# Loads and order of work in the head of a hybrid S5 / short-convolution layer

## The chip, the cores and the metric

The kernel runs on one core of one Trainium2 chip. The metric is device microseconds of one execution. TensorE (PE; its weight loads are listed as PEld), VectorE (DVE), ScalarE (ACT), GpSimd (POOL) and SyncE (SP) each work through an instruction list of their own, in order; the kernel is written so that the order of calls in the source is the order on every engine. Copies between device memory and the on-chip memory are issued by SP, ACT or POOL and run beside the engines.

## The reference, cut to what matters

One layer on a latent stream x (512 tokens by 2048 channels) and a context of 256 tokens:

```
shift, scale, gate = split(silu(c) @ w_ada + b_ada)       # the same with c_ctx for the context
h  = layernorm(x)   * (1 + scale)   + shift
hc = layernorm(ctx) * (1 + scale_c) + shift_c
u, z_s5, v, bg, cg, z_cv = split(h @ w_in);   u_c = hc @ w_in[:, :1024]
y_s5 = glu(s5_scan_both_directions(u, u_c))               # diagonal complex state space, 64 groups
y_cv = bg * conv3(cg * v)
x = layernorm(alpha * x + gate * (concat(y_s5 * silu(z_s5), y_cv * silu(z_cv)) @ w_out)) * ln_g + ln_b
```

All arithmetic is float32. A product with w_in, w_glu or w_out is made of three matmuls in a rounded format: both operands are split into a rounded part (hi) and the rest (lo), and hi·hi, lo·hi and hi·lo are summed.

## The kernel before, in words

The 2048 channels are 16 blocks of 128, numbered k. **The head** (`head`, line 461) makes the modulated, split input of every block (`hhi[k]`, `hlo[k]` for the 512 latent tokens, `chi[k]`, `clo[k]` for the 256 context tokens) and, in the same pass, the part of the input projection that needs the context: `lat` adds block k to three banks of latent u (9 matmuls of 512 columns), `cxt` to half of the context u (12 matmuls of 256 columns). A weight piece serves `cxt` for one half `hf` of the columns, and `lat` too where `hf` is 0; `half` (line 695) does one piece, two per k.

Rows of x and ctx come as six tiles of 128 rows (q = 0 to 3 of x, 4 and 5 of ctx). `stats` (524) takes mean and variance, `norm` (536) normalises in place, `turn` (554) transposes all 16 blocks through PSUM into `xl[k]` and `xc[k]`. The scale and shift of a block come from w_ada in 1 MB pieces (k, hf): `ada` (571) multiplies one piece with silu(c) in eight matmul calls that appear as 16 rows, into the tile `aps`; when both halves are in, `combine` (596) copies it (ACT, `part`), transposes it on PE into `cps`, reduces it on DVE into `ss[k]` and adds the bias `bss`. `aps` and `cps` are the two halves of one PSUM tile, and a write waits for the reads of the whole tile. `mod` (609) then computes hi on ACT and the two DVE steps that give lo.

The 1 MB pieces of w_ada and the four x tiles share a ring `wa` of RB = 7 buffers; the ctx tiles come as sixteen 128 KB pieces in another ring. `ada_ahead` (495) issues a piece of w_ada on POOL (the first on ACT) as soon as a buffer of the ring is given back. Weight pieces of 256 KB (`raw`, five buffers) are issued on SP by `load` (207). `ahead(i)` (214) splits the pieces up to two ahead of item i: `whi` on ACT, `wlo` on DVE, three buffers of each.

From k = 4 on a loop (705) repeats: `ada(k, 0)`, a `half`, `ada(k, 1)`, the first step of `combine`, a `half`, then `some(2.6)`, then the rest of `combine`, then `mod` for both streams. `some` (686) runs a stretch of `s5_params` (305): some two hundred small DVE steps that compute the discretised state-space parameters, cut at the `yield` lines; it stops when the planner's DVE clock has moved on by the given microseconds. Its sine and cosine, its quadrant step and its first power are blocks of around 20 instructions without a `yield`. Near its end it waits for the flag that `ada(13, 0)` is issued (then two ring buffers are free), transposes a table through `cps` in four steps and writes it to device memory (`Wd`). After the loop the last pieces run, then three u tiles are written out (`put_u`).

**The body** follows: 260 more items (256 KB weight pieces, nearly all with 12 matmuls of 512 columns) for the rest of the input projection, then the GLU, then the output projection. Beside them run background generators: `phase_w` (963, state inputs, from `Wd` and `bt`), the scan, `phase_y` (1086, outputs of the scan), `g_load` (1222) and the gate. The planner (`_Clock`, `_Timed`) keeps an estimated time for every engine and tile while the program is written; a background step is placed after the item at which the PE's estimated time has passed the estimated time of what it needs (`until`, `later`). Line 122 estimates when a copy has landed. The first GLU item (838) requires all of `g_load`.

Of the kernel before, what the change touches and what calls it, by code (L numbers as in the profile page):

```python
# [74 lines left out]
class _Timed:  # L75
# [26 lines left out]
    def __getattr__(self, what):  # L102
        f = getattr(self._e, what)

        def call(*a, **k):
            c, e = self._c, self._n
            out = a[0]
            ins = [x for x in list(a[1:]) + list(k.values()) if hasattr(x, "shape")]
            start = max([c.t[e]] + [c.free(out) - 0.13] + [c.ready(x) - (0.13 if c.who.get(c.key(x)) == e else 0.0) for x in ins])
            if what == "dma_start":  # L110
                if e == "pool":
                    c.t[e] = max(c.t[e], start - 1.5) + 1.0
                else:
                    c.t[e] = start if e == "sp" else c.t[e] + 0.5
                    c.hw = max(c.hw, min(start, c.t["pe"])) + 0.45
                    start = max(start, c.hw)
                n = 4
                for d in out.shape:
                    n *= d
                n *= min(2.0, max(1.0, 190.0 / min(out.shape[-1], ins[0].shape[-1]))) / 350e3  # L120
                c.bw = max(c.bw, min(start, c.t["pe"])) + n
                end = max(start + n, c.bw) + (4.0 if e == "pool" else 2.0)
            else:
                if e == "dve" and any(c.key(x) == c.last for x in ins):
                    start += 0.12
# [12 lines left out]

        return call
# [3 lines left out]
def tile_hybrid_s5_shortconv(  # L143
# [8 lines left out]
    ve, ac = _Timed(nc.vector, "dve", clk), _Timed(nc.scalar, "act", clk)  # L152
# [25 lines left out]
    def cslot(name, dt=F32):  # L178
        return hcp.tile([P, CTX], dt, name=name, tag="hc", bufs=32)
# [11 lines left out]
    def tt(out, a, b, op, e=None):  # L191
        (e or ve).tensor_tensor(out, a, b, op=op)
# [268 lines left out]
    def head():  # L461
        with pool(name="head", bufs=1) as hp, \
# [10 lines left out]
            ve.memset(epst, EPS)  # L473


            xt = {}

            def load_x(q):
                if q < 4:
                    t = hp.tile([P, D], F32, name="xt", tag="wa", bufs=RB)  # L480
                    n = 4 if q == 0 else 1
                    for f in range(n):
                        c = slice(f * D // n, (f + 1) * D // n)
                        sp.dma_start(t[:, c], x_in[q * P:(q + 1) * P, c])
                    xt[q] = [t[:, f * 512:(f + 1) * 512] for f in range(4)]
                else:
                    xt[q] = [cslot("xt") for _ in range(8)]
                    for f, t in enumerate(xt[q]):
                        sp.dma_start(t, ctx_in[(q - 4) * P:(q - 3) * P, f * CTX:(f + 1) * CTX])

            order = [(k, hf) for k in range(KT) for hf in range(2)]
            wa = {}
            nload = 0

            def ada_ahead(n):
                nonlocal nload
                while nload < min(n, len(order)):
                    t = hp.tile([P, D], F32, name="wa", tag="wa", bufs=RB)
                    (ac if nload == 0 else gp).dma_start(t, wada_ss[order[nload]])
                    wa[order[nload]] = t.rearrange("p (k c) -> p k c", k=8)  # L500
                    nload += 1

            for q in range(4):
                load_x(q)
            ada_ahead(RB - 4)
            for _ in range(2):
                load()
            for q in (4, 5):
                load_x(q)
            load()  # L510
            lam = hp.tile([P, 3, NG], F32, name="lam")
            for t, src in ((bss, b_ss), (lam, lam_in), (cvw, cv_w), (cvb, cv_b), (bgl, b_glu), (dsk, dsk_in)):
                sp.dma_start(t, src)
            acc = [ps.tile([P, 512], F32, name=f"acc{i}") for i in range(7)]
            aps = ps.tile([P, 512], F32, name="aps")
            aps, cps = aps[:, 0:256], aps[:, 256:512]
# [5 lines left out]
            sts, rss = {}, {}  # L522

            def stats(q):
                n = len(xt[q])
                stt = hp.tile([P, 8, 6], F32, name="bst", tag="bst", bufs=2)
                mv = hp.tile([P, 2], F32, name="mv", tag="mv", bufs=3)
                for f in range(n):
                    ve.bn_stats(stt[:, f], xt[q][f])
                    yield  # L530
                ve.bn_aggr(mv, stt[:, 0:n])
                sts[q] = mv
                rss[q] = rstd_a(hp, mv[:, 1:2], epst)
                yield

            def norm(q):
                yield from rstd_b(rss[q], sts[q][:, 1:2])
                for f, t in enumerate(xt[q]):
                    if q < 4:
                        if f:  # L540
                            break
                        t = bass.AP(tensor=t.tensor, offset=t.offset, ap=[t.ap[0], [1, D]])
                    ve.tensor_scalar(t, t, sts[q][:, 0:1], rss[q][:, 3:4], op0=OP.subtract, op1=OP.mult)

            def run(*gs):
                gs = list(gs)
# [5 lines left out]
                            gs.remove(g)  # L552

            def turn(q):
                w = 512 if q < 4 else CTX
                for k4 in range(4):
                    b = acc[(4 * q + k4) % 7 if q < 4 else 3 + k4]
                    for k in range(4):
                        c = (k4 * 4 + k) * P
                        pe.transpose(b[:, k * P:(k + 1) * P], xt[q][c // w][:, c % w:c % w + P], ident)  # L560
                    for k in range(4):
                        kk = k4 * 4 + k
                        dst = xl[kk][:, q * P:(q + 1) * P] if q < 4 else xc[kk][:, (q - 4) * P:(q - 3) * P]
                        if q == 5 and k % 2:
                            ve.tensor_copy(dst, b[:, k * P:(k + 1) * P])
                        else:
                            ac.activation(dst, b[:, k * P:(k + 1) * P], AF.Copy)
                if q < 4:
                    ada_ahead(RB - 3 + q)

            def ada(k, hf):
                w = wa.pop((k, hf))
                for j in range(8):
                    pe.matmul(aps[32 * (j % 4):32 * (j % 4) + 32], cs[:, hf * 8 + j], w[:, j],
                              start=hf == 0 and j < 4, stop=hf == 1 and j > 3)
                ada_ahead(2 * k + hf + RB + 1)
                done.add((k, hf))

            def lat(k, whi, wlo):
                lh, ll = hhi[k], hlo[k]  # L580
# [25 lines left out]
                ve.tensor_scalar(s[:, 1], s[:, 1], 1.0, None, op0=OP.add)  # L606
                yield

            def mod(k, x, his_, los_, new, m):
                his_[k], los_[k] = new("hi", F32R), new("lo", F32R)  # L610
                sh, sc = ss[:, k, 0, m:m + 1], ss[:, k, 1, m:m + 1]
                ac.activation(his_[k], x[k], AF.Identity, scale=sc, bias=sh)
                ve.tensor_scalar(x[k], x[k], sc, sh, op0=OP.mult, op1=OP.add)
                tt(los_[k], x[k], his_[k].bitcast(F32), OP.subtract)

            def mod_l(k):
                mod(k, xl, hhi, hlo, slot, 0)

            def mod_c(k):
                mod(k, xc, chi, clo, cslot, 1)  # L620

            def split(n):
                while st["split"] < n:
# [5 lines left out]
                    his[j] = (hi, lo)  # L629
                    st["split"] += 1  # L630

            done = set()
            run(stats(0))
            run(norm(0))
            run(stats(1))
# [45 lines left out]
            mod_l(3)  # L681
            mod_c(3)
            st["pos"] = 3
            params = s5_params(hp, cps, lam, lambda: (13, 0) in done)

            def some(us):
                t0 = ck["dve"]
# [16 lines left out]

            for k in range(4, KT):
                ada(k, 0)
                half()
                if k == 4:
                    half()
                ada(k, 1)  # L710
                next(comb[k])
                half()
                some(2.6)
                next(comb[k])
                mod_l(k)
                mod_c(k)
            while st["pos"] < 2 * KT:
                half()
                some(2.6)
# [742 lines left out]
```

## Time and profile before

| | |
|---|---|
| median of 3 runs | 1085.43 us (1080.07 to 1087.07) |
| profiled execution | 1081.24 us, span 1079.5 us |
| mean granted TensorE clock | 0.948 of full |
| busy: PE, PEld, DVE, ACT, POOL | 952.0, 764.4, 680.4, 374.3, 146.1 us |
| device memory | 179 GB/s mean over the span |

Busy time is what an engine's instructions took in the profiled execution, and the granted clock of 1.00 is 2.4 GHz, 0.50 is 1.2 GHz. PE is busy for 88% of the span, but not evenly: of the page's forty slices (27 us each) the second to ninth show it at 5 to 8 tenths, and the twelfth to the last but one at 8 or 9 tenths.

### The profile page before, as it was taken

Reading aid. Unit: us, or ns where it says so; the run is one execution under the profiler, and the core shown is the slowest. Engines: PE = TensorE matmul, PEld = TensorE weight load, DVE = VectorE, ACT = ScalarE, POOL = GpSimd, SP = SyncE. Lnnn points to the kernel's source line nnn. Section 1 sums busy time; section 2 is a strip of 40 time slices with the busy share of each in tenths; the row PEclk is TensorE's granted clock in tenths of the full one; section 3 lists DMA queues with packets and bytes.
Section 4 is the critical chain, followed back from the end, with each engine's and each line's share of the span. In section 5 each row is a group of like instructions: output and inputs, shape, how many; then the busy total and the mean of one; then the engine's idle time right before and its main releaser. Section 6 shows DMA issues by size and latency. Waiting matters only on the chain.

```text
span 1079.5 us, 15402 instructions
## 1 busy us (share of the span) xinstructions
PE 952.0 (88%) x5488; PEld 764.4 (71%) x5488; DVE 680.4 (63%) x1562; ACT 374.3 (35%) x669; POOL 146.1 (14%) x272
## 2 busy tenths in 40 slices
PE   1577776789699989999999999999989999999990
PEld 1455554568588877888888888888878887778780
DVE  4645555543487877898885667464124787982666
ACT  2432222223144334222424545444534442222321
POOL 1101003001011110000002021201020013300044
PEclk9879888789799999999999999999999999999996
DMA  9937555228999992333346364738397778945512
GB/s 326 377 121 281 206 185 216 79 59 197 234 220 215 217 233 83 107 108 113 108 142 175 126 177 131 174 110 187 92 272 228 238 242 303 307 155 152 158 59 97
DMA packets 106253, 194.53 MB, mean 180 GB/s; under 512 B 33600, under 2 KB 42944, under 8 KB 101568
## 3 DMA queue, kind: packets, MB, share of 16 engines
q1 hardware_dynamic: 71728, 107.14, 33.7%
q0 software_dynamic: 21616, 77.62, 24.3%
q10 hardware_dynamic: 12832, 8.78, 2.7%
q8 instruction: 43, 0.70, 0.3%
q14 instruction: 34, 0.28, 0.1%
HBM read 177.37 MB, written 16.12 MB: 179 GB/s over the span
## 4 chain that ended last, share of the span: by engine, by line
PE 73%; DVE 10%; DMA 9%; ACT 3%; issue 2%; SPq 1%; POOL 1%; ACTq 0%; DVEq 0%; POOLq 0%
PE mm L137 51%; PE bg L137 10%; PE acc L137 8%; PE aps L137 3%; DVE res L137 2%; DVE pt L137 2%; DMA raw<-in_w_m_dram 2%; DMA xt<-in_x_dram 2%; DMA pwt<-Wd 2%; DMA graw<-Gd 1%; DVE wlo L137 1%; DMA btt<-in_bt_dram 1%; DMA bss<-in_b_ss_dram 1%; ACT whi L137 1%; SPq L137 1%
## 5 line engine op out<-in xcount | busy, mean ns | idle before, releaser
L137 DVE TENSOR_TENSOR wlo<-raw,whi 128x512 fp32r<-128x512 f32 x276 | 187.5, 688 | 215.0 <-ACT whi L137 207.7
L137 PE MATMUL mm<-hi,wlo 128*128 128x512 f32 x720 | 283.6, 394 | 13.0 <-DVE wlo L137 12.9
L137 PE MATMUL mm<-hi,whi 128*128 128x512 f32 x720 | 286.4, 398 | 3.1 <-ACT whi L137 3.1
L137 PE MATMUL mm<-lo,whi 128*128 128x512 f32 x720 | 282.6, 393 | 0.0
L137 ACT ACTIVATE whi<-raw 128x512 fp32r<-128x512 f32 x276 | 171.1, 629 | 301.9 <-PE mm L137 220.4
L137 PEld LDWEIGHTS mm<-hi,wlo 128*128 128x128 f32 x720 | 136.6, 190 | 44.2 <-DVE wlo L137 15.2
L137 PEld LDWEIGHTS mm<-hi,whi 128*128 128x128 f32 x720 | 136.7, 190 | 35.2 <-ACT whi L137 4.1
L137 PEld LDWEIGHTS mm<-lo,whi 128*128 128x128 f32 x720 | 136.8, 190 | 27.5
L137 PE MATMUL aps<-wa,cs 128*32 128x256 f32 x512 | 39.8, 438 | 41.7 <-DVE ss L137 41.7
L137 PE MATMUL acc<-hi,whi 128*128 128x256 f32 (+1 forms) x176 | 65.7, 373 | 2.9 <-ACT hi L137 2.9
L137 PE MATMUL acc<-lo,whi 128*128 128x256 f32 (+1 forms) x176 | 61.1, 347 | 0.5 <-DVE lo L137 0.5
L137 PE MATMUL acc<-hi,wlo 128*128 128x256 f32 (+1 forms) x176 | 60.2, 342 | 0.0
L137 POOL DMA_DIRECT2D gw<-in_wada_g_dram x64 | 34.3, 538 | 150.5 <-DVE gacc L137 117.8
L137 PEld LDWEIGHTS aps<-wa,cs 128*32 128x32 f32 x512 | 14.8, 119 | 55.2 <-DVE ss L137 45.0
L137 PEld LDWEIGHTS acc<-hi,whi 128*128 128x128 f32 x176 | 38.1, 217 | 19.9 <-issue 13.5
L137 PE MATMUL acc<-ident,xt 128*128 128x128 f32 x96 | 18.5, 373 | 36.6 <-DVE xt L137 36.6
L137 DVE SCALAR_TENSOR_TENSOR gacc<-gw,cs,gacc 128x512 f32<-128x512 f32 x60 | 44.9, 749 | 1.2
L137 PEld LDWEIGHTS acc<-ident,xt 128*128 128x128 f32 x96 | 16.4, 196 | 38.8 <-DVE xt L137 33.4
L137 PEld LDWEIGHTS acc<-lo,whi 128*128 128x128 f32 x176 | 37.9, 215 | 4.1 <-DVE lo L137 1.0
L137 PEld LDWEIGHTS acc<-hi,wlo 128*128 128x128 f32 x176 | 37.3, 212 | 3.4
L137 POOL DMA_DIRECT2D wa<-in_wada_ss_dram x31 | 16.7, 540 | 162.0 <-PE aps L137 130.7
L137 POOL TENSOR_TENSOR res<-res,lnp 128x512 f32<-128x512 f32 x14 | 23.3, 1685 | 102.3 <-DVE res L137 99.8
(211 smaller groups left out, 1567.2 us busy)
## 6 DMA issues: line engine op xcount, KB each, us to landing
raw<-in_w_m_dram SPq DMA_DIRECT2D x180, 256.0 KB, 3.2
wa<-in_wada_ss_dram POOLq DMA_DIRECT2D x31, 1024.0 KB, 5.2
gw<-in_wada_g_dram POOLq DMA_DIRECT2D x64, 256.0 KB, 6.0
raw<-in_w_out_dram SPq DMA_DIRECT2D x64, 256.0 KB, 3.2
raw<-in_w_u_dram SPq DMA_DIRECT2D x32, 256.0 KB, 4.3
btt<-in_bt_dram POOLq DMA_DIRECT2D x16, 512.0 KB, 13.7
pwt<-Wd POOLq DMA_DIRECT2D x16, 512.0 KB, 12.5
uu<-Ud POOLq DMA_DIRECT2D x16, 384.0 KB, 7.4
```

The lines of the kernel that those rows point to most:

```text
L137: return f(*a, **k)
```

## The change

It touches only the head and one line of the planner. One list `ring` names the tiles of the 7-buffer ring in order of use: x 0 to 3, the first three pieces of w_ada, ctx tiles 4 and 5 as whole 1 MB tiles, the other pieces. `fill` issues the next one when the one seven places earlier has been used: x and ctx on SP, w_ada on POOL, except the first three pieces, which go on SP behind x. The six small loads (`bss`, `lam` and so on) go from SP to ACT. In the loop both `ada` calls of a k come first, the rest of `combine` comes between the two halves, and the parameter steps are cut in two: one stretch between the ACT and the DVE part of `mod`, one behind it. The planner expects copies issued by POOL or ACT to land 5 us after their transfer instead of 4 and 2; SP stays at 2.

```diff
-                end = max(start + n, c.bw) + (4.0 if e == "pool" else 2.0)
+                end = max(start + n, c.bw) + (2.0 if e == "sp" else 5.0)
...
-            for q in range(4):
-                load_x(q)
-            ada_ahead(RB - 4)
-            for _ in range(2):
-                load()
-            for q in (4, 5):
-                load_x(q)
-            load()
+            ring = [("x", q) for q in range(4)] + order[:3] + [("x", q) for q in (4, 5)] + order[3:]
+            rows, used = {}, set()
+
+            def fill(e=None):
+                while len(rows) < len(ring):
+                    n = len(rows)
+                    if n >= RB and ring[n - RB] not in used:
+                        return
+                    t = rows[ring[n]] = hp.tile([P, D], F32, name="wa", tag="wa", bufs=RB)
+                    a, b = ring[n]
+                    if a != "x":
+                        (e or gp).dma_start(t, wada_ss[a, b])
+                    elif b == 0:
+                        for f in range(4):
+                            sp.dma_start(t[:, f * 512:(f + 1) * 512], x_in[0:P, f * 512:(f + 1) * 512])
+                    else:
+                        sp.dma_start(t, x_in[b * P:(b + 1) * P] if b < 4 else ctx_in[(b - 4) * P:(b - 3) * P])
+
+            fill(sp)
+            for _ in range(3):
+                load()
...
-                sp.dma_start(t, src)
+                ac.dma_start(t, src)
...
             def stats(q):
-                for f in range(n):
-                    ve.bn_stats(stt[:, f], xt[q][f])
+                for f in range(4):
+                    ve.bn_stats(stt[:, f], rows["x", q][:, f * 512:(f + 1) * 512])
...
             def norm(q):
-                for f, t in enumerate(xt[q]):
...
+                t = rows["x", q]
+                ve.tensor_scalar(t, t, sts[q][:, 0:1], rss[q][:, 3:4], op0=OP.subtract, op1=OP.mult)
...
-                if q < 4:
-                    ada_ahead(RB - 3 + q)
+                used.add(("x", q))
+                fill()
...
-                ada_ahead(2 * k + hf + RB + 1)
-                done.add((k, hf))
+                used.add((k, hf))
+                fill()
...
+            def mod(k, parts, between=None):
+                for x, hi, lo, new, m in parts:
+                    hi[k], lo[k] = new("hi", F32R), new("lo", F32R)
+                    ac.activation(hi[k], x[k], AF.Identity, scale=ss[:, k, 1, m:m + 1], bias=ss[:, k, 0, m:m + 1])
+                if between:
+                    between()
+                for x, hi, lo, new, m in parts:
+                    ve.tensor_scalar(x[k], x[k], ss[:, k, 1, m:m + 1], ss[:, k, 0, m:m + 1], op0=OP.mult, op1=OP.add)
+                    tt(lo[k], x[k], hi[k].bitcast(F32), OP.subtract)
...
             for k in range(4, KT):
                 ada(k, 0)
+                ada(k, 1)
+                next(comb[k])
                 half()
                 if k == 4:
                     half()
-                ada(k, 1)
                 next(comb[k])
                 half()
-                some(2.6)
-                next(comb[k])
-                mod_l(k)
-                mod_c(k)
+                mod(k, [lpart, cpart], lambda: some(1.3))
+                some(1.3)
```

## Rows read from the trace of the kernel before

**Rows 1.** Stretches: length, busy (count) of PE, PEld, DVE, ACT, POOL; clock; DMA; GB/s.

```profile
33.90:58.00 24.10, 12.70 (x110) 9.46 (x109) 12.48 (x39) 9.62 (x48) 3.32 (x6) 0.79 0.89 353
...
87.20:96.80 9.60, 6.83 (x73) 5.29 (x73) 6.17 (x23) 2.85 (x5) 1.06 (x2) 1.00 0.95 336
96.80:109.25 12.45, 9.13 (x67) 6.42 (x67) 6.53 (x25) 2.73 (x5) 1.06 (x2) 0.86 0.72 266
...
226.90:239.30 12.40, 10.45 (x75) 7.04 (x76) 3.61 (x8) 4.27 (x9) 0.00 (x0) 0.87 0.15 44
...
248.90:1040.00 791.10, 774.81 (x4255) 631.78 (x4254) 525.43 (x1117) 299.14 (x474) 101.57 (x206) 0.99 0.64 177
```

**Rows 2.** PE's waits from 96.8 to 227 us: total, times, longest.

```profile
PE aps L137 <- DVE ss L137: 39.2, 11, 4.4
```

**Rows 3.** Timeline, about one k: start, duration, instruction, idle before and releaser.

```profile
100.86 0.39 PE L137 MATMUL acc<-hi,whi 128*128 128x512 f32 x1
101.09 0.39 PE L137 MATMUL acc<-lo,whi 128*128 128x512 f32 x1
...
102.48 0.28 PE L137 MATMUL acc<-hi,wlo 128*128 128x256 f32 x1
102.59 0.28 PE L137 MATMUL acc<-hi,whi 128*128 128x256 f32 x1
...
103.03 1.07 PE L137 MATMUL aps<-wa,cs 128*32 128x256 f32 x16
...
105.16 0.69 DVE L137 TENSOR_TENSOR wlo<-raw,whi 128x512 fp32r<-128x512 f32 x1 [4.49 <-ACT whi L137]
...
109.03 0.17 DVE L137 TENSOR_REDUCE ss<-aps 128x4 f32<-128x16 f32 x1
...
109.25 1.07 PE L137 MATMUL aps<-wa,cs 128*32 128x256 f32 x16 [3.32 <-DVE ss L137]
...
110.48 0.55 DVE L137 TENSOR_SCALAR xl<-xl,ss 128x512 f32<-128x512 f32 x1 [0.88 <-ACT hi L137]
...
111.02 0.63 PE L137 MATMUL acc<-hi,wlo 128*128 128x512 f32 x1
...
111.45 0.63 PE L137 MATMUL acc<-hi,whi 128*128 128x512 f32 x1
...
112.45 0.68 DVE L137 TENSOR_TENSOR wlo<-raw,whi 128x512 fp32r<-128x512 f32 x1
```

**Rows 4.** DVE instructions by form, 96.7 to 227 us: busy, mean ns, idle before.

```profile
L137 DVE SCALAR_TENSOR_TENSOR pt<-pt,pt 128x64 f32<-128x64 f32 x21 | 4.7, 225 | 0.7
```

**Rows 5.** Timeline of PE at the parameter table's transposes.

```profile
237.29 0.44 PE L137 MATMUL aps<-ident,PI 128*128 128x128 f32 x2 [0.47 <-ACT WT L137]
```

**Rows 6.** Timeline from the start to 51 us.

```profile
7.46 0.69 DVE L137 BATCH_NORM_STATS2 bst<-xt 128x6 f32<-128x512 f32 x1 [6.12 <-DMA xt<-in_x_dram]
...
16.04 1.34 DVE L137 BATCH_NORM_STATS2 bst<-xt 128x6 f32<-128x512 f32 x2 [0.93 <-DMA xt<-in_x_dram]
...
19.07 1.34 DVE L137 TENSOR_SCALAR xt<-xt,mv,sd 128x2048 f32<-128x2048 f32 x1
...
34.17 1.30 SPq L137 DMA_DIRECT2D cvb<-in_cv_b_dram  x1
...
42.84 0.16 DVE L137 TENSOR_TENSOR ss<-ss,bss 128x4 f32<-128x4 f32 x1 [1.94 <-DMA bss<-in_b_ss_dram]
...
50.84 2.66 DVE L137 TENSOR_SCALAR xt<-xt,mv,sd 128x256 f32<-128x256 f32 x8
```

**Rows 7.** DMA queues in the first 8 us: packets, MB, share of 16 engines.

```profile
q1 hardware_dynamic: 2216, 0.30, 35.9%
q0 software_dynamic: 117, 0.93, 32.1%
```

**Rows 8.** By tile: durations min/median/max in ns, first and last start in us.

```profile
L137 DVE TENSOR_TENSOR glo<-graw,ghi x8: 684/692/695, 791.6 to 818.3; 128x512 fp32r<-128x512 f32 x8
...
L137 SPq DMA_DIRECT2D Zd<-cvv x8: 423/425/560, 739.7 to 831.1; - x8
```

More of the change, by code (lines that the diff above doesn't have):

```diff
@@ L473, in head @@
             ve.memset(epst, EPS)
-            xt = {}
-            def load_x(q):
-                if q < 4:
-                    t = hp.tile([P, D], F32, name="xt", tag="wa", bufs=RB)
-                    n = 4 if q == 0 else 1
-                    for f in range(n):
[L483 to L487, printed above, removed]
-                    for f, t in enumerate(xt[q]):
-                        sp.dma_start(t, ctx_in[(q - 4) * P:(q - 3) * P, f * CTX:(f + 1) * CTX])
@@ L491, in head @@
-            order = [(k, hf) for k in range(KT) for hf in range(2)]
[L492 to L501, printed above, removed]
-            for q in range(4):
-                load_x(q)
@@ L524, in stats @@
             def stats(q):
-                n = len(xt[q])
-                stt = hp.tile([P, 8, 6], F32, name="bst", tag="bst", bufs=2)
+                stt = hp.tile([P, 4, 6], F32, name="bst", tag="bst", bufs=2)
                 mv = hp.tile([P, 2], F32, name="mv", tag="mv", bufs=3)
-                for f in range(n):
-                    ve.bn_stats(stt[:, f], xt[q][f])
+                for f in range(4):
+                    ve.bn_stats(stt[:, f], rows["x", q][:, f * 512:(f + 1) * 512])
                     yield
-                ve.bn_aggr(mv, stt[:, 0:n])
+                ve.bn_aggr(mv, stt)
                 sts[q] = mv
@@ L537, in norm @@
                 yield from rstd_b(rss[q], sts[q][:, 1:2])
[L538 to L543, printed above, removed]
+                t = rows["x", q]
+                ve.tensor_scalar(t, t, sts[q][:, 0:1], rss[q][:, 3:4], op0=OP.subtract, op1=OP.mult)
             def run(*gs):
@@ L554, in turn @@
             def turn(q):
-                w = 512 if q < 4 else CTX
+                t = rows["x", q]
                 for k4 in range(4):
@@ L558, in turn @@
                     for k in range(4):
-                        c = (k4 * 4 + k) * P
-                        pe.transpose(b[:, k * P:(k + 1) * P], xt[q][c // w][:, c % w:c % w + P], ident)
+                        kk = k4 * 4 + k
+                        pe.transpose(b[:, k * P:(k + 1) * P], t[:, kk * P:(kk + 1) * P], ident)
                     for k in range(4):
@@ L567, in turn @@
                             ac.activation(dst, b[:, k * P:(k + 1) * P], AF.Copy)
-                if q < 4:
-                    ada_ahead(RB - 3 + q)
+                used.add(("x", q))
+                fill()
             def ada(k, hf):
-                w = wa.pop((k, hf))
+                w = rows[k, hf].rearrange("p (k c) -> p k c", k=8)
                 for j in range(8):
@@ L607, in combine @@
                 yield
[L609 to L614, printed above, removed]
+            def mod(k, parts, between=None):
[7 more added lines that the diff above has]
+                    tt(lo[k], x[k], hi[k].bitcast(F32), OP.subtract)
+            lpart, cpart = (xl, hhi, hlo, slot, 0), (xc, chi, clo, cslot, 1)
             def mod_l(k):
-                mod(k, xl, hhi, hlo, slot, 0)
+                mod(k, [lpart])
             def mod_c(k):
-                mod(k, xc, chi, clo, cslot, 1)
+                mod(k, [cpart])
             def split(n):
@@ L630, in split @@
                     st["split"] += 1
-            done = set()
             run(stats(0))
@@ L683, in head @@
             st["pos"] = 3
-            params = s5_params(hp, cps, lam, lambda: (13, 0) in done)
+            params = s5_params(hp, cps, lam, lambda: (13, 0) in used)
             def some(us):
```

## The prediction

> **What bounds the kernel now.** I read the busy time by stretches first. From 248.9 to 1040 us PE is busy for 774.8 of 791.1 us: the body is paced by PE, and the change gives PE no less to do there. Before that, a k of the loop lasts 12.45 us with 9.13 us of PE and 6.53 us of DVE, and the granted clock is 0.86, which lies between the two levels of 1.2 and 2.4 GHz [rows 1]. So neither engine is full in the loop: each waits for the other. The waits of PE name the place: 39.2 us in 11 waits, all of the first `ada` of a k for `ss` on DVE [rows 2]. One k in order of time shows why. DVE has nothing to do for 4.49 us until `whi` of the second half comes, because that ACT copy stands behind `part`, and `part` behind `ada(k, 1)`. Then DVE does `wlo` and 3.3 us of parameters (from the end of `wlo` at 105.8 to 109.03), and only then the reduction that frees the shared PSUM tile; PE has been idle for 3.32 us when it goes on at 109.25 [rows 3]. After such a gap the 512-column matmuls start every 0.43 us (111.02 to 111.45) instead of every 0.23 us (100.86 to 101.09) [rows 3]: the gap is paid a second time in the clock.
>
> From the first k of the loop (87.2) to the end of the twelfth (239.3) it takes 152.1 us [rows 1], where the first and the last of the twelve stand. That is the stretch in which the change has most to win. Ahead of it lie 87 us in which rows are normalised and transposed.
>
> **The change, part by part.**
>
> *Order of the loop.* After it, reduction k stands on DVE right behind the transposes, and the second half's 12 matmuls cover it before the next `ada` needs the tile. The wait of 3.3 us goes; what is late next is found from the three loads on a k.
> PE at the upper clock: two `ada` of 1.0 us (103.03, less the pipelined tail), nine matmuls at 0.23 and 24 at 0.11 to 0.12 (102.48 to 102.59) make 2.0 + 2.1 + 2.8 us [rows 3]; with 0.3 for the transposes and 0.4 for switching, 7.6 us.
> DVE: two `wlo` of 0.65, the sums 0.6, the four steps of `mod` 2.0 (110.48 to 112.45), parameters 3.3 [rows 3]: 7.2 us. The 0.88 us in which DVE waited for ACT's hi now holds parameters.
> Copies: 2.10 MB of w_ada and 0.52 MB of weights at the 353 GB/s of the busiest stretch [rows 1]: 7.4 us, and the ring runs 3.5 k ahead, so a slow copy is covered by some 25 us of work; without that cover the k would be at least 7.4 us anyway.
> The three are close, so I take PE's 7.6 and 0.2 for hand-overs: 12 x 7.8 = 93.6 us. Five things are added: the extra half of k = 4, 1.4 us. The parameter blocks without a `yield`: about 20 instructions of 0.21 us (225 ns for the commonest [rows 4]) are 4.2 us, not 1.3; three of them come in two consecutive k, DVE has 12.5 and 9.6 us to do there, and PE then waits some 4 and 2.5 us, 6.5 together, with 2 us for the clock behind it. The four transposes of the parameter table stay a chain of PE and ACT, 4 x 0.91 = 3.6 us [rows 5]. Sum 107.1 us instead of 152.1: **-45 us**. Bounds: 12 x 7.6 + 1.4 + 3.6 = 96 us (-56), and 9.5 us a k, a DVE that still loses half of its present 4.49 us, with the same additions, 127.5 (-25).
> What POOL issues in the loop is the same two copies a k; the ACT part of `mod` doesn't move against `whi`.
>
> *x first.* Now the 256 KB pieces of x 0 share the engines with 1 MB pieces of w_ada: after 8 us the SP queue has moved 0.30 MB and POOL's 0.93 [rows 7]. The first statistics start at 7.46, the last two at 16.04 [rows 6]. With w_ada behind x on SP, the 1.23 MB that have landed by 8 us hold all of x 0 (1.05 MB), so the last piece's statistics start at 8.0 instead of 16.7: 8.7 us, and the rows behind it keep their pace because DVE has been busy without a break since (1.34 us for norm 0 at 19.07 [rows 6], and so on to q = 3). Bounds: 0, if the pieces land no sooner, and 9.5.
>
> *Small loads.* The first modulation waits 1.94 us for `bss` [rows 6], which SP issues after the sixteen ctx pieces; issued by ACT at the start it is there: -1.9. The six issues cost ACT what they cost SP, at most 1.30 us each [rows 6], in a stretch where ACT's next work, the first square root, is due at about 9 us; they cover 4 to 8 us of it. If they run longer, the root is late by at most 3 us; I take 0. The Trainium skill (DMA: Bandwidth & Descriptors, Issuing engines are not separate DMA queues) says the opposite of a gain: issuing on several engines saves only the sequencer's time, the transfers interleave anyway. By it the wait of 1.94 us would stay.
>
> *ctx as whole tiles.* They lose one thing: norm 4 was 8 steps of 0.33 us (2.66 in all [rows 6]), PE started after the first, and the four statistics woven into its square root were half as long. Now PE waits for 1.34 us of norm and 1.3 us more of statistics, less some slack: +1.9 us at q = 4, +0.7 at q = 5. They also arrive later, behind 8.1 MB on SP and only when x 0 is transposed: 9.2 MB at 353 GB/s is 26 us, about 29 with the start, and up to 36 where POOL's pieces take half of the engines; needed at about 35. So 0 to +4; I take 0. SP holds weight pieces 4 and on behind the ctx tiles; nobody needs them before 80 us.
>
> Head ahead of the loop: -8.7 - 1.9 + 1.9 + 0.7 = **-8.0 us** (bounds -11 and +2).
>
> *Planner line.* It changes where the body's background steps are placed, not their work. Of PE's 16.3 idle us in the body [rows 1] later placing can save at most that. Against it, in `phase_y` a copy by ACT (3 us later) and one by POOL (1 us) follow each other in each of eight blocks, two blocks under way: 16 us later in all, to 32 without overlap. Then `g_load` ends 16 us later than its 819.0 (818.3 + 0.69), while the first GLU item may start when the last z piece is done, shortly before its copy at 831.1 [rows 8]: 12 us are free, 4 to 20 us would be PE's. Between -13 and +20 I take 0, as the small loss and the gain of a first stall lie close.
>
> Sum: 1081.24 - 45 - 8 + 0 = **1028 us**. That is against the profiled execution's own time (span 1079.5 and 1.7 around it), 4.2 us under the median of 1085.43, inside the spread of the three runs; I write 1029.
>
> **Rivals.**
> 1. *DVE takes PE's place in the loop.* Its work, 7.2 us, is nearly PE's 7.6, and `wlo` still stands ahead of the reduction. For it: 4.49 us of waiting for ACT now. Against: `whi` of the first half depends on nothing late any more. If half of that wait stays, k = 9.5 and the kernel 1049; if all, 11.7 us a k, 154 us, 1075.
> 2. *The clock stays at the lower level in the loop.* The matmuls then start at 0.43 us, twice the time: 13.3 us a k, 12 x 13.3 and 9 for the same additions at that clock, 168.6, 16.5 us more than now, less 8: **1089.7, slower than before**. It decides from 12.4 us a k on. Against it: at full speed PE would have no gap near the present 3.32 us, and the body, with no such gap, shows 0.99 [rows 1]. The Trainium skill (TensorE: Matmul & The Clock Gate, A second HAM failure mode: psum-queue depth-cycling) describes a kernel whose short pauses between matmul groups alone kept the clock moving between the levels. By that rule the switches between `ada`, halves and transposes would do it; the stretch 87.2 to 96.8, which has the same switches and one wait, shows 1.00 [rows 1].
> 3. *The background is stretched past its slack.* 30 us too late instead of 4 makes 1055. The gain would be gone only at 12 + 53 = 65 us of delay, more than phase_y's 32.
> 4. *The x pieces land no sooner.* Then the early gain is lost: 1037.
>
> **Chances.** A measurement here tells about 1%, 10.8 us, from no change. Forecast 0.60; DVE with half its wait 0.17, with all of it 0.05; the clock 0.04; the background 0.07; x no sooner 0.07. Faster by over 1% (under 1070): 0.60 + 0.17 + 0.07 + 0.07, less 0.01 for a mix of losses, 0.90. Within 1%: 0.05 + 0.02 of the clock's = 0.07. Slower: 0.03 for the clock's upper end and the unseen. Range: the forecast's bounds from the sums are 1001 and 1050 (-56 - 11 - 13, and -45 + 2 + 12 where only one loss is large); I take 1007 to 1055, which holds rivals 3 and 4 and the milder half of rival 1.
>
> **What would show it.** The loop's k at 7.6 to 8.2 us, with two or three longer ones; `ada` waiting for `ss` under 10 us in all instead of 39.2; the clock at 1.00 through the loop; the first transposes at about 12 us, the loop starting at about 79 and the body at about 196; no wait for `bss`. Wrong would be: `wlo` still waiting 4 us for `whi`; the k at 12 us or more; PE idle for more than 5 us ahead of the first GLU item; statistics of q = 4 waiting for their tile.

## The result, and the profile after

The median is 1021.91 us (four runs, 1019.75 to 1022.81), against 1083.51 for the kernel before in the same session: a ratio of 0.9428, interval 0.9391 to 0.9466. The forecast was 1029. The profiled execution took 1022.81 us (span 1021.0, mean clock 0.969), 58.4 less than the 1081.24 of the one before.

Where these 58 us come from is read from three moments of TensorE: its first transposes, the `ada(4, 0)` that begins the loop, and the first matmul of the body (`mm`).

| us | before | after | difference | forecast |
|---|---|---|---|---|
| start to first transposes | 20.47 | 15.79 | -4.7 | -8.7 |
| from there to the loop | 66.72 | 67.82 | +1.1 | +0.7 |
| loop to first body matmul | 161.97 | 109.98 | -52.0 | -45 |
| body to the end of the span | 830.3 | 827.4 | -2.9 | 0 |

The loop in busy time by stretches, columns as in [rows 1]: before, from its start to the first body matmul, and after.

```profile
87.19:249.16 161.97, 120.85 (x881) 88.69 (x882) 83.62 (x277) 38.66 (x71) 15.18 (x33) 0.84 0.48 167
```

```profile
90.05:97.19 7.14, 7.14 (x68) 5.71 (x67) 6.13 (x23) 2.81 (x6) 1.07 (x2) 1.00 1.01 415
114.07:125.99 11.92, 8.68 (x68) 6.14 (x68) 11.10 (x55) 2.84 (x5) 1.06 (x2) 0.87 0.66 223
83.61:193.59 109.98, 101.15 (x881) 79.82 (x882) 82.61 (x277) 39.83 (x71) 15.75 (x33) 0.95 0.67 246
```

The same 881 matmuls and 277 VectorE instructions now take 110 us. VectorE's busy time has hardly changed; TensorE's fell by 19.7 us, because at the upper clock the same matmul is shorter (mean granted clock 0.95 instead of 0.84). A plain k (first row) is 7.14 us with TensorE busy throughout and a clock of 1.00, where [rows 1] had 12.45 us at 0.86. The second row is the worst k. Its VectorE column says why it lasts 11.92 us: 55 instructions of 11.10 us, against 23 of 6.13.

The waits of TensorE from 83 to 176 us (total, times, longest); the first row answers to [rows 2], which covered 11 k.

```profile
PE aps L137 <- DVE ss L137: 7.6, 4, 3.2
PE aps L137 <- ACT WT L137: 2.5, 4, 1.1
```

Time lines of VectorE and TensorE at one of these four waits. The steps on `pt` are the parameters; the first row begins a block without a `yield`, the fourth ends it.

```profile
109.00 0.22 DVE L137 TENSOR_TENSOR pt<-lam,pt 128x64 f32<-128x64 f32 x1
109.25 0.66 DVE L137 TENSOR_SCALAR pt<-pt 128x64 f32<-128x64 f32 x3
...
113.13 0.19 DVE L137 TENSOR_SCALAR pt<-pt 128x64 f32<-128x64 f32 x1
113.24 0.69 DVE L137 TENSOR_TENSOR wlo<-raw,whi 128x512 fp32r<-128x512 f32 x1
113.85 0.17 DVE L137 TENSOR_REDUCE ss<-aps 128x4 f32<-128x16 f32 x1
```

```profile
114.07 2.36 PE L137 MATMUL aps<-wa,cs 128*32 128x256 f32 x20 [2.52 <-DVE ss L137]
```

The block holds VectorE from 109.00 to 113.3. `wlo` and the reduction stand behind it, and TensorE waits 2.52 us for the reduction. That is the wait of the loop before, now mostly where a long block falls: 2.52 and 3.24 us stand behind long blocks, 0.59 behind a shorter stretch of parameters, and 1.29 belong to the first `ada` of the loop, ahead of any parameters, as at 87.19 before.

The start, in order of time (ACTq is an issue of a copy); it answers to [rows 6].

```profile
4.09 0.38 ACTq L137 DMA_DIRECT2D bss<-in_b_ss_dram  x1
...
6.28 0.34 ACTq L137 DMA_DIRECT2D lam<-in_lam_dram  x1
6.28 2.81 DVE L137 BATCH_NORM_STATS2 bst<-wa 128x6 f32<-128x512 f32 x4 [4.95 <-DMA wa<-in_x_dram]
6.96 0.33 ACTq L137 DMA_DIRECT2D cvw<-in_cv_w_dram  x1
7.63 0.42 ACTq L137 DMA_DIRECT2D cvb<-in_cv_b_dram  x1
8.40 0.33 ACTq L137 DMA_DIRECT2D bgl<-in_b_glu_dram  x1
9.13 0.26 DVE L137 BATCH_NORM_AGGREGATE mv<-bst 128x2 f32<-128x24 f32 x1
11.37 0.34 ACTq L137 DMA_DIRECT2D dsk<-in_dsk_dram  x1
11.73 1.28 ACT L137 ACT_TABLE_LOAD   x1 [6.18 <-DMA wa<-in_x_dram]
13.03 0.30 ACT L137 ACTIVATE sd<-mv,epst 128x1 f32<-128x1 f32 x1
13.36 0.17 DVE L137 RECIPROCAL sd<-sd 128x1 f32<-128x1 f32 x1 [3.97 <-ACT sd L137]
```

All statistics of x 0 are finished at 9.39 us, where the last two began at 16.04 before [rows 6]. But the square root `sd` runs only at 13.03: ACT issues the six small loads ahead of it, the last at 11.37, and the table load for the root (1.28 us), which ran at 5.52 before, comes behind them.

### The profile page after: what moved, and what is told of

Its sections match the earlier page's. It is cut to its first block, busy times and chain, and to the rows that moved or that the text cites. A ratio compares the mean times of both kernels' runs of the same rounds, so it can differ in the third digit from the quotient of the medians.

```text
span 1021.0 us, 15369 instructions
## 1 busy us (share of the span) xinstructions
PE 933.2 (91%) x5488; PEld 755.1 (74%) x5488; DVE 674.8 (66%) x1540; ACT 378.9 (37%) x671; POOL 146.6 (14%) x270
## 4 chain that ended last, share of the span: by engine, by line
PE 68%; DVE 14%; DMA 10%; issue 4%; ACT 2%; SPq 0%; ACTq 0%; POOL 0%; DVEq 0%; POOLq 0%
PE mm L137 50%; PE bg L137 10%; PE acc L137 6%; DMA Ud<-ut 4%; DMA btt<-in_bt_dram 3%; DVE res L137 3%; PE aps L137 2%; DVE wlo L137 2%; DVE pt L137 2%; DVE tm L137 1%; DMA pwt<-Wd 1%; DVE bst L137 1%; DMA graw<-Gd 1%; DVE lo L137 1%; DMA wa<-in_x_dram 1%
## 5 line engine op out<-in xcount | busy, mean ns | idle before, releaser
L137 PE MATMUL mm<-hi,wlo 128*128 128x512 f32 x720 | 283.6, 394 | 10.5 <-DVE wlo L137 10.3
L137 PE MATMUL acc<-hi,whi 128*128 128x256 f32 (+1 forms) x176 | 59.6, 338 | 2.9 <-ACT hi L137 2.9
L137 PE MATMUL acc<-lo,whi 128*128 128x256 f32 (+1 forms) x176 | 56.7, 322 | 0.5 <-DVE lo L137 0.5
L137 PE MATMUL acc<-hi,wlo 128*128 128x256 f32 (+1 forms) x176 | 56.0, 318 | 0.0
L137 PE MATMUL acc<-ident,wa 128*128 128x128 f32 x96 | 18.8, 378 | 32.3 <-DVE wa L137 32.3
L137 PE MATMUL aps<-wa,cs 128*32 128x256 f32 x512 | 35.1, 415 | 9.4 <-DVE ss L137 8.9
L137 PEld LDWEIGHTS acc<-hi,whi 128*128 128x128 f32 x176 | 34.5, 196 | 12.1 <-issue 5.0
L137 PEld LDWEIGHTS acc<-ident,wa 128*128 128x128 f32 x96 | 17.0, 202 | 34.4 <-DVE wa L137 28.1
L137 PEld LDWEIGHTS acc<-lo,whi 128*128 128x128 f32 x176 | 34.5, 196 | 3.2 <-DVE lo L137 1.0
L137 PEld LDWEIGHTS acc<-hi,wlo 128*128 128x128 f32 x176 | 34.6, 197 | 2.3
L137 ACT ACTIVATE hxx<-vst 64x512 f32<-64x512 f32 x32 | 36.2, 1130 | 0.3
```

## Experiments

"Before" and "after" are the two kernels; a ratio is to the kernel before in the same session. "Loop" below is the time from `ada(4, 0)` to the first body matmul of the profiled execution: 162.0 us before, 110.0 after.

**The loop without the loads:** before, with the loop and `mod` of after.

```diff
+            def mod(k, parts, between=None):
...
                 ada(k, 0)
+                ada(k, 1)
+                next(comb[k])
                 half()
...
-                some(2.6)
...
+                mod(k, [lpart, cpart], lambda: some(1.3))
+                some(1.3)
```

> Before, with the loop of the change alone (both ada of a k first, the rest of combine between the halves, the parameters in two stretches behind the sums); loads and planner as before. Theory: the loop is the gain; it takes about 101 us instead of 152.1, so about 1032 us, and nothing ahead of 87 us changes. Rival: the new ring is needed to feed so short a k; then the k stays above 9 us and the kernel above 1050.

Ratio 0.9488 (0.9423 to 0.9553); loop 107.2 us, first transposes at 20.54 as before. The new order of the loop by itself gives nearly the whole gain, so it does not need the new ring (the rival).

**The loads without the loop:** after, with the loop and `mod` of before.

```diff
                 ada(k, 0)
-                ada(k, 1)
-                next(comb[k])
                 half()
...
+                ada(k, 1)
...
+                some(2.6)
                 next(comb[k])
-                mod(k, [lpart, cpart], lambda: some(1.3))
-                some(1.3)
+                mod_l(k)
+                mod_c(k)
```

> After, with the old loop: the ring in order of use, the small loads on ACT and the planner's line remain. Theory: 3.6 us from the start and 3 from the body, about 1077 us, the k still at 12.7. Rival, as first forecast: 8 us from the start, 1072 or less.

Ratio 0.993 (0.9879 to 0.9981), 1073.26 us; first transposes at 15.72, loop start at 82.57, waits for `ss` 40.2 us in 12. The loads bring 4 to 5 us of head, and the loop is no shorter (165.1 us). The body of this execution is 8.7 us shorter than before; that belongs to what is left open at the end.

**Only the parameters moved, `ada` still apart,** in before.

```diff
-                some(2.6)
                 next(comb[k])
                 mod_l(k)
                 mod_c(k)
+                some(2.6)
```

> Before, with one line moved: some(2.6) goes behind mod instead of ahead of the rest of combine; the second ada stays between the halves. Theory that the parameters ahead of the reduction make the wait: PE waits under 1 us a k for ss, k about 8.2, about 1037 us. Rival, that the second ada between the halves holds back whi and with it all of DVE: k about 11, 1065 us.

Ratio 0.9602 (0.9493 to 0.9712), median 1039.79 us. Waits of TensorE in its loop and one of its k, views as above (the profiled execution, 1027.96 us, was the fastest of the four):

```profile
PE aps L137 <- DVE ss L137: 9.2, 13, 1.4
```

```profile
94.98:102.80 7.82, 7.55 (x68) 5.64 (x68) 6.19 (x23) 2.74 (x5) 1.06 (x2) 1.00 0.93 350
```

Nothing but the place of the parameters, and the waits fall from 40 to 9 us, the loop from 162.0 to 113.1.

**Only `ada` together, the parameters ahead of the reduction as in before;** the rest is after.

```diff
                 half()
+                some(2.6)
                 next(comb[k])
                 half()
-                mod(k, [lpart, cpart], lambda: some(1.3))
-                some(1.3)
+                mod(k, [lpart, cpart])
```

> After, with the parameters put back ahead of the reduction (some(2.6) before the rest of combine, none in mod); both ada of a k stay together. Theory that the parameters ahead of the reduction make the wait: the reduction comes 3.3 us later, and as the second half covers 1.4 us and ada needs it at the end of that, PE waits about 1 to 2 us a k: about 1040 us. Rival, that having both ada first is enough, because DVE gets wlo early: under 0.5 us a k, within 4 us of 1022.

Ratio 0.9449 (0.9352 to 0.9547); its loop is 105.3 us, with

```profile
PE aps L137 <- DVE ss L137: 7.3, 9, 1.3
```

So either of the two moves takes nearly all of the wait away. Before, the reduction was late by the wait for `whi` and by the parameters one behind the other [rows 3]; with either out of the way the rest nearly fits under TensorE's matmuls. The two gains of the loop, 49 us (parameters moved) and 57 us (`ada` together), do not add: both moves gave 52.0 us in after, and 55 where its new loop stood alone. Cutting the parameters in two adds nothing that could be measured once the two `ada` are together; with the parameters in one piece there are nine waits of at most 1.3 us, and the clock is 1.00 over the whole loop.

**After again, and its planner line undone.**

> The change once more, as the measure for the three kernels run with it: 1022 us, ratio 0.943.

Ratio 0.9422 (0.9383 to 0.9461), 1019.26 us; body 825.1 us.

```diff
-                end = max(start + n, c.bw) + (2.0 if e == "sp" else 5.0)
+                end = max(start + n, c.bw) + (4.0 if e == "pool" else 2.0)
```

> After, with the planner's line as before (POOL copies 4 us, ACT copies 2). Theory that the later due times are where the body's 2.9 us come from: 1025 us, PE's waits in the body back near those of before. Rival: the body's difference is chance of placement, 1022 within 2 us.

Ratio 0.9457 (0.9425 to 0.949), body 827.0 us: no difference that can be told. Together with the body's 830.3 and 827.4 us before and after, the planner line is worth nothing here, within 2 or 3 us.

**The six small loads on POOL.**

```diff
-                ac.dma_start(t, src)
+                gp.dma_start(t, src)
```

> After, with the six small loads issued by POOL instead of ACT. Theory: on ACT the sixth load waits for the landing of x 1 (11.4 us) and the first square root stands behind it; on POOL nothing does, the root comes at about 9.7 instead of 13.0 and the loop starts 3.6 us earlier: 1018 us. Rival: the root waits for the table load whoever issues the small loads, or the head waits for x 1 anyway: 1022.

Ratio 0.9321 (0.929 to 0.9351), 1008.27 us: clearly faster than after. ACT's time line at the start:

```profile
5.56 1.28 ACT L137 ACT_TABLE_LOAD   x1
10.64 0.29 ACT L137 ACTIVATE sd<-mv,epst 128x1 f32<-128x1 f32 x1 [3.80 <-DVE mv L137]
```

The table is loaded early, the root waits for nothing but VectorE, and the first transposes come at 13.40 instead of 15.79. POOL issues the six loads from 2.00 to 4.84 us, one every 0.53. But the span is 14 us shorter than after's: the loop starts 2.5 us sooner and is 2.8 shorter, at a clock of 0.98 instead of 0.95, the end behind the last store is 4.4 shorter, which is told further down, and the body up to that store is 4.3 shorter, which stays open.

**The first three w_ada pieces on POOL.**

```diff
-            fill(sp)
+            fill()
```

> After, with the first three w_ada pieces issued by POOL at the start instead of by SP behind x. Theory that the order of use brought x 0 early: the last statistics of x 0 start at about 16 instead of 8.3 us, the first transposes 4 to 8 us later, 1026 us. Rival: the order within the queues matters little, 1022.

Ratio 0.9442 (0.9404 to 0.948), no change in the total, but a different course. Its DMA queues in the first 8 us (packets, MB, share of 16 engines) and those of after:

```profile
q0 software_dynamic: 150, 1.14, 44.3%
q1 hardware_dynamic: 2188, 0.26, 24.8%
```

```profile
q1 hardware_dynamic: 2658, 1.22, 62.1%
```

With w_ada on a queue of its own, the x queue has moved 0.26 MB by 8 us, as before [rows 7], against 1.22: with w_ada behind x in SP's list, the 16 engines move x 0 first. In after a wait helps: SP's first w_ada piece goes out only at 14.14 us, with the small loads on POOL at 5.96 (SP's issues, after and that kernel):

```profile
14.14 2.93 SPq L137 DMA_DIRECT2D wa<-in_wada_ss_dram  x3
```

```profile
5.96 2.04 SPq L137 DMA_DIRECT2D wa<-in_wada_ss_dram  x3
```

The statistics of x 0 end at 9.39 us in after, at 10.61 with the small loads on POOL and at 17.21 here. So the place behind x in one queue is most of the gain; the late issue in after may be the rest, though with the small loads on POOL these too (0.14 MB) move in the first 11 us. ACT's issues here, same view as above:

```profile
9.20 0.34 ACTq L137 DMA_DIRECT2D lam<-in_lam_dram  x1
12.39 0.34 ACTq L137 DMA_DIRECT2D cvw<-in_cv_w_dram  x1
15.54 0.34 ACTq L137 DMA_DIRECT2D cvb<-in_cv_b_dram  x1
...
18.78 0.33 ACTq L137 DMA_DIRECT2D dsk<-in_dsk_dram  x1
...
20.44 0.30 ACT L137 ACTIVATE sd<-mv,epst 128x1 f32<-128x1 f32 x1
```

The same issues, up to 8 us later than in after, with x landing later and the ACT list unchanged. So ACT does not work through them at a pace of its own: it waits for copies issued by SP ahead of them. The trace's semaphores (the counters by which a copy reports that it has landed) say which: each of the five behind `bss` waits for the counter on which it will itself report, and a load of x reports on the same one. In after the four quarters of x 0 have landed at 6.26, 6.94, 7.61 and 8.38 us and x 1 at 11.35, each 0.02 us ahead of one of the five issues; the first w_ada piece waits in the same way for x 2, landed at 14.12. The first transposes come at 23.19 and the body starts 6.6 us later than in after, yet the end is no later: the time behind the last store is 4.6 us shorter, for the reason told below, and the body up to it 2.7 shorter. So the unchanged total hides a slower head.

**More `yield` lines inside the long parameter blocks:** eight in all, of which two are shown.

```diff
         stt(r, k, -7.54978995489188e-8, r, OP.mult, OP.add)
+        yield 0
         tt(z, r, r, OP.mult)
...
         tt(s, s, r, OP.add)
+        yield 0
         ts(c, z, 2.443315711809948e-5, -1.388731625493765e-3, OP.mult, OP.add)
```

> After, with an extra yield inside each of the eight long blocks of the S5 parameters, so that a block of 4 us on VectorE is handed out in two. Theory (the parameter blocks are what still makes the halves of ada late): the 7.6 us that TensorE waits for ss in the loop fall under 2, the clock of 0.86 between 115 and 135 us rises to 0.97, 5 to 8 us less than after: ratio to before 0.935 to 0.938. Rival (VectorE has the same sum of work, and what does not wait in one k waits in the next, as where the parameters stand ahead of the rest of the combine: 9 waits of 7.3 us for 4 of 7.6): within 1.5 us of after, ratio 0.942 to 0.945.

Ratio 0.9332 (0.9294 to 0.937), 1010.22 us: 0.9% under after. Stretch from loop start to body, and waits from 84 to 200 us:

```profile
83.38:182.60 99.22, 96.32 (x882) 78.11 (x883) 81.57 (x277) 39.98 (x71) 16.68 (x33) 1.00 0.75 272
```

```profile
PE aps L137 <- DVE ss L137: 1.3, 1, 1.3
```

The loop falls from 110.0 to 99.2 us at a clock of 1.00, with the same instructions. My rival, that the waiting would only move to other k, was wrong. (The wait of 1.27 us ahead of the loop's first `ada`, at 83.38, is not in this view; it is in the 7.6 us of after.) The gain is more than the wait that it removes, 10.8 us for 5.1: TensorE's busy time also fell, by 4.8 us, at the higher clock. Not all of that need be the `yield` lines: five other kernels with after's loop take 107.2 us for it, at a higher clock (told below under the rivals), so 8.0 to 10.8 us are theirs.

**Only x 4 normalised ahead of its transposes.**

```diff
-            run(norm(4), stats(5))
+            run(norm(4))
             turn(4)
+            run(stats(5))
```

> After, with norm(4) alone ahead of turn(4) and stats(5) behind it. Theory (TensorE's 7.8 us idle before turn(4) are VectorE's, which puts the four statistics of q=5, 4 x 0.6 us, between the pieces of norm(4)): turn(4) 2.4 us earlier, and the loop start with it: ratio 0.940. Rival (what stands behind turn(4), the lat and ada work, waits for the modulation and not for turn(4), and stats(5) is late for turn(5) instead): start of the loop within 0.5 us of after, ratio as after, 0.942 to 0.944.

Ratio 0.9411 (0.9365 to 0.9457), by itself not to be told from after. In the trace, TensorE's wait in front of these transposes is shorter: after, and this kernel.

```profile
46.66 3.68 PE L137 MATMUL acc<-ident,wa 128*128 128x128 f32 x16 [7.77 <-DVE wa L137]
```

```profile
44.55 3.67 PE L137 MATMUL acc<-ident,wa 128*128 128x128 f32 x16 [4.62 <-DVE wa L137]
```

Counted from the first transposes, the loop starts 2.0 us sooner (65.78 against 67.82 us). The theory holds in size, under what the times resolve.

**One small load, `dsk`, on POOL.**

```diff
-                ac.dma_start(t, src)
+                (gp if t is dsk else ac).dma_start(t, src)
```

> After, with one of the six small loads, dsk, on POOL instead of ACT. In after its issue came last on ACT, at 11.37 us, 3.0 after the one ahead of it. Theory A (ACT's root of the first statistics waits behind the issues, the last of them by 3 us): the root comes at 10.0 to 10.7 instead of 13.0, the first transposes at 12.8 to 13.4, 2.4 us less. For the end of the program: with POOL's first DMA issue at 2 us, the two kernels so far ended 3.4 us behind the last store, the other eight, with the first at 30 us or later, 8 us, POOL's last drain taking 2.4 to 2.6 or 10.8 to 10.95 us. Theory B (one early issue on POOL is enough for the short end): another 4.5 us less, 7 in all, ratio 0.936. Rival to B (it is the number of issues on POOL, 57 and 54 of which gave the short end, 51 the long one): 52 issues, the long end, ratio 0.940.

Ratio 0.9388 (0.9341 to 0.9436). ACT's last issue, its table and the root:

```profile
8.87 0.34 ACTq L137 DMA_DIRECT2D bgl<-in_b_glu_dram  x1
9.24 1.28 ACT L137 ACT_TABLE_LOAD   x1 [3.68 <-DMA wa<-in_x_dram]
10.53 0.29 ACT L137 ACTIVATE sd<-mv,epst 128x1 f32<-128x1 f32 x1
```

Theory A holds: the root at 10.53, the first transposes at 13.29. One issue, the one that waited longest, was nearly all of the delay. For the end of the program theory B fell: the early issue on POOL did not shorten it.

What the end goes with then came out of a count over all kernels. (The counts in the expectation, 57, 54, 51 and 52, are wrong: the profile's lists of issues give 195, 192, 189 and 190.) Behind the last store, the program waits for a DRAIN of POOL, the longest of three in these rows (count, min/median/max in ns, first and last start in us). After, then the kernel with three w_ada pieces on POOL:

```profile
L1442 POOLq DRAIN  x3: 51/97/10782, 1009.5 to 1020.8; - x3
```

```profile
L1442 POOLq DRAIN  x3: 51/98/2370, 1013.3 to 1020.0; - x3
```

| copies issued by POOL | longest DRAIN, us | kernels | last store issued to end |
|---|---|---|---|
| 189 | 10.78 | after and its variants | 8 |
| 190 | 10.87 | `dsk` on POOL | 8 |
| 191 | 10.95 | before and its variants | 8.4 |
| 192 | 2.37 | three w_ada pieces on POOL | 3.3 |
| 195 | 2.61 | six small loads on POOL, and the last kernel below | 3.5 |

The DRAIN grows by 0.083 us for each copy and falls by 8.6 us between 191 and 192; the program then ends 4.5 us sooner behind its last store. All fourteen profiled executions fit. Theory B had its answer in the kernel before: POOL issues two w_ada pieces there at 2.00 us, not at 30, and the end is long. In every one of these kernels the total is 189 plus the copies that POOL issues in the first 5 us (0, 1, 2, 3 or 6), so no run tells whether the total or these early copies decide, and none shows why the DRAIN falls.

**The three together:** small loads on POOL, the extra `yield` lines, x 4 alone.

> After with the three edits together that helped by themselves: the six small loads on POOL, the extra yields in the parameter blocks, and norm(4) alone ahead of turn(4). If they add: the small loads 0.0101 of the ratio (0.9422 to 0.9321), the yields some 0.009 to 0.011, norm(4) 0.001 to 0.003, from 0.942: 0.918 to 0.922, about 994 us, the first transposes at 13.4, the first matmul of the body at 176 to 178 us, and with 57 issues on POOL its last drain under 3 us. Rival (once the loop and the start are shorter, the body's first weights wlo, or the DMA queues, which were above 0.9 busy in the loop, take the gain back): 0.928 to 0.932, as the small loads or the yields alone, with TensorE's waits for wlo in the body above 15 us instead of 10.

Ratio 0.9225 (0.9187 to 0.9263), 1000.84 us, faster than both kernels and than each edit alone. Stretch from loop start to body, and waits of the body:

```profile
78.94:178.13 99.19, 96.27 (x882) 78.06 (x882) 81.56 (x277) 39.99 (x71) 16.64 (x33) 1.00 0.76 273
```

```profile
PE mm L137 <- DVE wlo L137: 11.8, 4, 5.8
```

Against the profiled execution of after: the loop starts 4.7 us sooner, the loop is 10.8 shorter, the end 4.5 shorter, the body to its last store 0.6 shorter; 20.5 in all. The three edits add, within the interval. The wait for the first weights of the body, 10.3 us in after, stays.

## Why the prediction was right, and where its steps were off

*Order of the loop (forecast -45, measured -52).* Right, and for the reason given: `ss` was the late link, and in the k without a gap the clock is at its upper level. The main mis-sized term is the plain k. I added 0.3 for the transposes and 0.4 for switching to TensorE's 6.9 us of matmuls and 0.2 for hand-overs, 7.8 in all; a plain k is 7.14 us with no idle time, so both costs lie mostly inside the pipelined times already counted. Twelve times 0.66 is 7.9 us. The extra half of k = 4 had the wrong sign: I added 1.4 us for it, but the three halves of that k are pieces with `hf` = 1, which have no `lat`, and it takes 6.44 us (83.61 to 90.05), 0.7 less than a plain k. Against these 10.0 us stand 3.0. Four k are 2.60, 4.78, 1.59 and 0.66 us over the plain one, 9.6 us against the 8.5 I gave the long blocks and the clock behind them; with the finer yields one k of 8.49 us is left of it. The k with the table's transposes is 4.1 over, against 3.6, and from the start of the last k to the body it takes 18.4 us, 1.4 more than a plain k and the 9.9 behind the twelfth k before. The four transposes still follow each other at 0.91 us (after, time line of TensorE):

```profile
173.34 0.44 PE L137 MATMUL aps<-ident,PI 128*128 128x128 f32 x2 [0.47 <-ACT WT L137]
```

What I did not see: that for the old order either of two moves is nearly enough. I priced the change as a whole, and its edits would have been priced wrongly one by one.

*x first (-8.7, measured -4.7).* This is the step that was off, in the term that I set to 0: "If they run longer, the root is late by at most 3 us; I take 0." The data came as forecast: the statistics of x 0 end at 9.39 us. But ACT's six issues were not 1.30 us each; each took 0.33 to 0.42, five of them waited before that for copies of SP, and the table load stood behind them, so the root came 3.6 us late. The bound of 3 came from the durations of such issues on SP [rows 6], and a duration does not contain what the issue waits for.

*`bss` (-1.9) and ctx (+2.6).* The first modulation no longer waits. It is gone because `bss` is issued at 4.09 us instead of at 32.42 behind the ctx pieces, so it was the place in a list that counted, more than the faster landing (4.5 us behind the issue instead of 10.3). The Trainium skill (DMA: Bandwidth & Descriptors, Issuing engines are not separate DMA queues) states that issuing on several engines saves only the sequencer's time to issue. The trace agrees with that; that the wait would stay by it, as I wrote, does not follow, since a place in a list is just such time. Of the head's remainder, the transposes of q = 4 come 4.6 us sooner than before and those of q = 5 3.3 us, that is 2.0 and 1.4 us of the early gain of 6.6 given back, against 1.9 and 0.7; the kernel with x 4 alone shows the first of these as VectorE's statistics in TensorE's way. The ctx tiles were not late.

*Planner line and body (0).* Right within 3 us, by the kernel with the old line. The last GLU copy and the last z piece are 56 and 58 us earlier and keep their order (after, by tile; they answer to [rows 8]), and TensorE waits 0.3 us there instead of 2.8:

```profile
L137 DVE TENSOR_TENSOR glo<-graw,ghi x8: 685/692/693, 739.6 to 762.5; 128x512 fp32r<-128x512 f32 x8
...
L137 SPq DMA_DIRECT2D Zd<-cvv x8: 327/426/508, 686.9 to 773.1; - x8
```

*Rivals.* VectorE did not take TensorE's place: no plain k waits for it. The clock did not stay down: the plain k have the same switches between `ada`, halves and transposes and show 1.00, so there the rule of the Trainium skill (TensorE: Matmul & The Clock Gate, A second HAM failure mode: psum-queue depth-cycling) did not decide. But it was not 1.00 through the whole loop, as I had expected. It was 0.87 and 0.80 in the two k behind the waits for VectorE of 2.52 and 3.24 us, and 0.76 in the k behind the table's transposes, where TensorE had waited four times for ACT (0.47 to 1.05 us). The second and third of these stretches in after, then in the kernel with x 4 alone, whose waits are nearly as long (3.16 us; 0.47 to 1.01):

```profile
125.99:134.72 8.73, 8.73 (x67) 6.63 (x68) 7.54 (x23) 3.51 (x6) 4.97 (x12) 0.80 0.33 98
175.16:182.25 7.09, 7.09 (x54) 4.60 (x55) 0.69 (x1) 0.90 (x2) 0.00 (x0) 0.76 0.36 92
```

```profile
124.06:131.21 7.15, 7.15 (x67) 5.71 (x68) 6.74 (x22) 2.85 (x5) 4.39 (x10) 1.00 0.25 74
172.15:179.20 7.05, 7.05 (x68) 5.75 (x68) 1.80 (x5) 2.11 (x4) 0.00 (x0) 1.00 0.41 114
```

The loop takes 110.0 us where the clock falls there (after, after again, three w_ada pieces on POOL) and 107.2 where it does not (the loop alone, the old planner line, small loads on POOL, x 4 alone, `dsk` on POOL). The wait for VectorE was 3.24 to 3.27 us in the three and 3.02 to 3.22 in the five; the waits for ACT were the same in some of both (1.05 to 1.06 and three of 0.47 us, also with the old planner line and with the small loads on POOL). So the same loop has two courses of 2.8 us difference; what chooses between them, and whether the page's rule is at work behind the transposes, no run shows.

The x pieces did land sooner. The errors of +4.4 in the head, -7.0 in the loop and -2.9 in the body make the 5.5 us between the sum of 1028 and the execution of 1022.8. That the sum came so close is in part luck: what the head lost and what the loop gained over the forecast cancel.

*Left open.* From its first matmul to its last store the body took 810.8 to 819.5 us in kernels whose body is the same. The waits for first weights differ between them (8.0 us with `dsk` on POOL, 13.2 in after), but that explains only part of it. No run tells the rest.

## What to carry to other kernels

Where a result is late by two things in a row on an in-order engine, and either alone would fit under the other engine's work, moving one can be enough: price the combinations, not the edits. A long block without a cutting point can cost more than its own wait, where the clock falls behind the gap; finer cutting of work that is already placed took 0.9% off here. When a copy's issue is moved to another engine, ask what the issue itself waits for and what stands behind it, not only how long issues last.

## What the runs showed of the hardware that was not expected

- An issue of a small load on ACT can be held for microseconds by copies that another engine issued: `dsk` went out at 11.37 us, 2.97 behind the issue ahead of it and 0.02 behind the landing of x 1, and at 18.78 where x landed later. SP's first w_ada piece was held in the same way, to 14.14 us instead of 5.96. The same six issues on POOL, ahead of its other copies, went out every 0.52 to 0.72 us.
- The DRAIN of POOL at the end of a program took 10.78 to 10.95 us behind 189 to 191 copies issued by POOL, and 2.37 to 2.61 behind 192 and 195, worth 4.5 us at the end of the span. The total and the number of copies issued at the start are not separated.
- With the queues at 415 GB/s for a whole k (90.05 to 97.19), no copy was late in the loop: the 353 GB/s that the forecast took from the busiest stretch before [rows 1] was not a ceiling; the page of before already has a slice at 377.
- Behind the same four waits of TensorE for ACT (one of 1.05 or 1.06 us, three of 0.47) its clock in the next k was 0.76 to 0.78 in three executions and 1.00 in two; three more, with 0.97 to 1.05 us for the first, also show 1.00.
